# Gate weights loaded one step ahead of their product, into two buffers, over the scan's sixteen units

## The chip, the core and the metric

One core of a Trainium2 chip runs the whole layer. The engines are TensorE (PE in the profile; its weight loads are PEld), VectorE (DVE), ScalarE (ACT), GpSimd (POOL) and SyncE (SP), whose queue issues every DMA of this kernel. The metric is the device time of one execution in microseconds (us).

## What is computed

One layer of a hybrid backbone on 512 tokens of width 2048, with 256 context tokens, in float32. Cut to what matters here:

```
shift, scale, gate = split(silu(c) @ w_mod + b_mod, 3)
p = (rmsnorm(x, norm_g) * (1 + scale) + shift) @ w_in      # q, k, v, g, z, x|B|C, dt
y = bi_ssd(conv_silu(x|B|C), softplus(dt), ...)             # scan, both directions, 4 groups, 16 heads
a = windowed_gqa(rope(q), rope(k), v, context k and v, sink)
h = concat(rmsnorm(a * silu(g)), rmsnorm(y * silu(z)))
out = rmsnorm(x + gate * (h @ w_out), final_norm_g)
```

`gate` is a row of 2048 numbers, a product of one vector with a 2048 x 2048 part of `w_mod`. It is needed only in the output projection, at the end.

## The kernel before

Every product with weights runs on TensorE in three parts (hi x hi, lo x hi, hi x lo), so each weight block is split first: ScalarE rounds it to `wh` (L308), VectorE forms the rest `wl` (L310, counted under the helper's L55). Weights of the input projection come in units of 128 columns (`load_unit`, L298): two loads of 512 KB (`wr`, L303, two buffers), each split in two quarters (four buffers of `wh` and `wl`). Unit 0 is the last z block. Units 1 to 16 belong to the scan: for each of four groups two units of x, one of B, one of C (L598). Units 17 and 18 are the keys, then come queries and gates of the attention. x, B, k units multiply latent and context tokens (`pj` and `pjc` in the profile), C and q units the latent tokens alone.

After the four units of a group its scan follows (`ssd_group`, L474): the convolutions (L465 to L472), transposes, the chain of chunk states (`stc`, `stx`, L515 to L531), and for each of two head pairs the decays `df` (DMA broadcast L562, four buffers; ScalarE exp L563, L569, L573; VectorE L566, L575) and the output `yps` on TensorE (L586), which waits for them. While a scan runs, TensorE fills its time with the next group's first units, so much of them as its order allows.

The gate row is worked off in 64 steps among all this (`gate_step`, L274), one for each quarter of the units 2 to 17 (L311). A step loads 128 x 512 weights (`wg`, L289, 256 KB, **one** buffer) and adds their product with one column of silu(c) to an accumulator `ga` on VectorE (L290). The load is queued on SP behind the unit's own weight load (`issue_after`). Sixteen steps make one accumulator of 512 columns; after the sixteenth TensorE sums it over partitions (`gp`, L293), ScalarE copies the row (L294), SP stores it (L295), and POOL clears the one accumulator buffer for the next (L283).

A planner of the language fixes at build time the order of every engine's queue: each engine takes the earliest instruction of the program that is ready by the planner's own estimate of durations. `high_priority` puts weights (L301, by 200 instructions), convolutions (L461, 200) and the `df` loads (L561, 150) ahead. On the chip each queue then runs strictly in that order: an instruction that waits holds all behind it on its engine.

Of the kernel before, what the change touches and what calls it, by code (L numbers as in the profile page):

```python
# [6 lines left out]
F32 = mybir.dt.float32  # L7
# [5 lines left out]
PSUM = bass.MemoryType.PSUM  # L13

P = 128
D = 2048
KT = 16
# [6 lines left out]
GB = 1  # L24
# [11 lines left out]

# columns of the packed constants
C_ID, C_SEL, C_AP, C_AN, C_TRI, C_TRIT, C_MF, C_MB, C_END = 0, 128, 130, 258, 386, 514, 642, 770, 898
# columns of the packed small parameters
V_NG, V_BSH, V_BSC, V_CW, V_CB, V_DSK, V_AG, V_SG, V_DTB, V_ALOG, V_SINK, V_C, V_END = (  # L40
# [3 lines left out]
def emit(tc, xin, ctxT, wmod, wgate, bgate, wz, wvd, wu, wo, fng, vecs, cst, rope, out, dbg=None):  # L44
    nc = tc.nc
# [17 lines left out]
    with es:  # L63
# [7 lines left out]

# [1 line left out]
        c_sb = pc.tile([P, P + 2], F32, name="c_sb")  # L73
# [13 lines left out]

        # persistent activations: transposed normalised inputs in two exact parts
        cy = es.enter_context(tc.tile_pool(name="cy", bufs=1))
# [17 lines left out]
        def silu2(src, o, tmp):  # L107
            """o = 2 * src * sigmoid(src) = src * (1 + tanh(src / 2))"""
            nc.scalar.activation(tmp, src, AF.Tanh, scale=0.5)
            nc.vector.scalar_tensor_tensor(out=o, in0=tmp, scalar=1.0, in1=src, op0=ALU.add, op1=ALU.mult)  # L110

# [1 line left out]
        sus = ExitStack()  # L113
        su = sus.enter_context(tc.tile_pool(name="su", bufs=2, side="right", reuse_waits="tile"))

        def rms_rows(o, acc, n, tag):
            """1 / rms of every token, on all partitions, from the sums of squares per partition."""
            nt = n // P
            tot = bank(tag, f"rtot_{n}", shape=(P, nt))
            for t in range(nt):  # L120
                mm(tot[:, t:t + 1], acc[:, t * P:(t + 1) * P], ones[:, 0:1], True, True)
            rs = sp.tile([P, nt], F32, tag="rsc", name=f"rs_{n}")
            rstd_of(rs, tot, D)
            rps = bank(tag, f"rps_{n}", shape=(P, n))
            for t in range(nt):
                dg = sp.tile([P, P], F32, tag="dg", name=f"dg_{n}_{t}", bufs=4)
                nc.vector.tensor_scalar(out=dg, in0=ident, scalar1=rs[:, t:t + 1], scalar2=None, op0=ALU.mult)
                mm(rps[:, t * P:(t + 1) * P], ones, dg, True, True)
            nc.scalar.activation(o, rps, AF.Copy)

        def load_latent():
            """Latent tokens: transposed as they come, in column blocks; 1 / rms of every token on all partitions."""
            xtags = ["mm", "sa", "tp", "mm", "sa", "tp", "mm"]
# [3 lines left out]
            for q in range(4):  # L137
# [8 lines left out]
                for i in range(4):  # L146
                    k = 4 * q + i
# [28 lines left out]

        # silu of the two modulation vectors, zero-padded to one column group
        scp = su.tile([P, KT, 32], F32, tag="scp", name="scp", bufs=1)
# [87 lines left out]

# [1 line left out]
        dp = es.enter_context(tc.tile_pool(name="dp", bufs=1, space=bass.MemoryType.DRAM))  # L268
        grow = dp.tile([1, D], F32, name="grow")
        gsteps = iter(range(4 * KT))  # L270
        gacc = []
        geng = nc.vector

        def gate_step(ld):  # L274
            """One k block of 512 gate columns: products per partition, summed over partitions after the last."""
            i = next(gsteps, None)
            if i is None:
                return
            n, k = divmod(i, KT)
            if k == 0:  # L280
                ga = wp.tile([P, 512], F32, tag="ga", name=f"ga_{n}", bufs=1)
                gacc.append(ga)
                nc.gpsimd.memset(ga, 0.0)  # L283
                with tc.issue_after(ld.ins):
                    nc.sync.dma_start(ga[0:1, :], bgate[:, n * 512:(n + 1) * 512])
            ga = gacc[n]
            wg = wp.tile([P, 512], F32, tag="wg", name=f"wg_{n}_{k}", bufs=GB)
            with tc.issue_after(ld.ins):
                nc.sync.dma_start(wg, wgate[n, k])  # L289
            geng.scalar_tensor_tensor(out=ga, in0=wg, scalar=sc0[:, k:k + 1], in1=ga, op0=ALU.mult, op1=ALU.add)  # L290
            if k == KT - 1:
                gp = bank("tp", f"gp_{n}", shape=(1, 512))
                mm(gp, ones[:, 0:1], ga, True, True)  # L293
                nc.scalar.activation(ga[0:1, :], gp, AF.Copy)  # L294
                nc.sync.dma_start(grow[:, n * 512:(n + 1) * 512], ga[0:1, :])  # L295

# [1 line left out]
        def load_unit(u, ctxp=False):  # L298
            """Yields (k, hi, lo) weight blocks [128, 128] of unit u."""
            for hf in range(2):  # L300
                with tc.high_priority(HP_W):  # L301
                    wr = wp.tile([P, 8, P], F32, tag="wr", name=f"wr_{u}_{hf}", bufs=WR)
                    ld = nc.sync.dma_start(wr, wu[u, :, hf * 8:hf * 8 + 8, :])  # L303
                for qf in range(2):
                    with tc.high_priority(HP_W):
                        wh = wp.tile([P, 4, P], F32R, tag="wh", name=f"wh_{u}_{hf}_{qf}", bufs=4)
                        rr = wr[:, qf * 4:qf * 4 + 4, :]
                        nc.scalar.activation(wh, rr, AF.Copy)  # L308
                        wl = wp.tile([P, 4, P], F32R, tag="wl", name=f"wl_{u}_{hf}_{qf}", bufs=4)
                        tt(nc.vector, wl, rr, f32(wh), ALU.subtract)  # L310
                    if 2 <= u < 18:  # L311
                        gate_step(ld)
                    for i in range(4):
                        yield hf * 8 + qf * 4 + i, wh[:, i, :], wl[:, i, :]
# [14 lines left out]

# [1 line left out]
        def xtk(t, k):  # L331
# [61 lines left out]

# [1 line left out]
        sst = ExitStack()  # L395
# [6 lines left out]
        def w2(name, tag="w2", bufs=4, shape=(P, S)):  # L402
            return sd.tile(list(shape), F32, tag=tag, name=name, bufs=bufs)
# [5 lines left out]

        # dt: softplus(u) = max(u,0) + log1p(exp(-|u|)), log1p(e) = 2 atanh(e / (2 + e))  # L410
        fl = [P, 192]
# [47 lines left out]
        def conv_silu(pa, pb, ci, o):  # L459
            """Depthwise conv of width 3 and silu: pa [128, n] in PSUM -> o in SBUF."""  # L460
            with tc.high_priority(HP_CONV):  # L461
# [12 lines left out]
        def ssd_group(g, units):  # L474
# [65 lines left out]
            for pr in range(2):  # L540
                tix = 2 * g + pr
                # state term of both heads at once: exp(cs) scales it afterwards
                zs = []
# [9 lines left out]
                for hh in range(2):  # L553
# [3 lines left out]
                    for d in range(2):  # L557
                        # the row of running sums on all partitions; the differences take its place
                        df = w2(f"df_{r}_{d}", "df", DF)
# [20 lines left out]
                    dm.append(dx[0])  # L580
                # the two heads' products alternate between the two column halves of the array
                for c in range(NT):
# [12 lines left out]

        # units: (xs0 xs1 B C) x 4, k0 k1, q x 8, g x 8
        U0 = 8 - NZ
# [9 lines left out]

# [1 line left out]
        ast = ExitStack()  # L609
# [18 lines left out]

        # keys: scaled by 1/8 once (exact)
        kT = [a2(f"kT_{i}", "kT", 2, (P, S + CT)) for i in range(2)]  # L630
# [6 lines left out]

        # context activations are no longer needed: their room takes the SSD hi part and the attention output
        attT = [cy.tile([P, 2, S], F32, tag=f"cb{j}", name=f"at{j}") for j in range(4)]
        rsum = pc.tile([P, 2, NT], F32, name="rsum")  # L640

        def finish_half(src, hi_pair, goff, which, lo_tiles, pool, tag, bufs, apool, atag):
            """Sum of squares per token; norm gain; split in two parts."""
            acc = apool.tile([P, S], F32, tag=atag, name=f"hacc_{which}")
# [139 lines left out]

# [1 line left out]
        px_s.close()  # L786
# [12 lines left out]
        def add_x(n):  # L799
            """part = part * gate + x for 512 columns"""  # L800
            nn = slice(n * 512, (n + 1) * 512)
# [8 lines left out]
        for half in (1, 0):  # L810
# [6 lines left out]
            for n in range(4):  # L817
# [45 lines left out]
                for t in range(NT):  # L863
# [4 lines left out]
                    if last:  # L868
                        tmp = fp.tile([P, 512], F32, tag="xo", name=f"lt_{t}", bufs=4)
                        rt = rf[:, t:t + 1]  # L870
                        # the very last block in two column halves, so that only the second one's epilogue is left over
                        cut = [0, 512] if t < NT - 1 else [0, TC, 512]
# [137 lines left out]
```

## Time and profile before

| | us |
|---|---|
| median of 3 runs | 1056.75 |
| lowest, highest | 1056.4, 1060.85 |
| span of the profiled execution | 1054.8 |
| TensorE busy in that span | 1009.6 |
| VectorE busy | 722.0 |
| ScalarE busy | 494.6 |

The profiled execution's own time is its span, from its first to its last instruction; the median of the runs is 1.95 us above it, for what lies around the span. TensorE's busy time is modelled from its pipeline, so the idle time and the granted clock of a stretch say more than the share. In the rows below a bracket after a row of a timeline gives the engine's idle time before that row and what ended it.

### The profile page before, as it was taken

The page shows a single profiled execution, that of the slowest core. Times are in us where ns is not written, and L with a number is a line of the kernel's source. Part 1 is how long each engine was busy: PE and PEld are TensorE (multiplying, and loading weights), DVE is VectorE, ACT ScalarE, POOL GpSimd, SP SyncE. Part 2 cuts the span into 40 slices and gives each one's busy share as a digit, 9 for nine tenths or more (in the row PEclk, how much of TensorE's full clock was granted, in tenths as well). Part 3 has the DMA queues.
Part 4 walks back from the last instruction along what each step waited for, and adds up shares of the span by engine and source line. Part 5 has one row for each costly group of instructions (what it writes and reads, how often), then busy time and mean ns, then how long its engine had stood idle before and what let it go on. Part 6 is the DMA issues. An engine that isn't in the chain of part 4 may idle for free.

```text
span 1054.8 us, 15524 instructions
## 1 busy us (share of the span) xinstructions
PE 1009.6 (96%) x5682; PEld 818.7 (78%) x5682; DVE 722.0 (68%) x1474; ACT 494.6 (47%) x1064; POOL 173.5 (16%) x120
## 2 busy tenths in 40 slices
PE   5999999999999989989989999999999998999996
PEld 4677789788778868868868777777777777888885
DVE  4332378585875985885889888788798866333765
ACT  6222275263352453263345567666666655333333
POOL 1232200000210110110037100000000008744220
PEclk9999999999999999989999999999999999999998
DMA  9999963354244244444331211112111135442304
GB/s 333 385 347 348 343 212 95 110 165 147 70 120 145 92 149 125 112 120 139 120 107 56 84 61 42 59 40 80 41 40 61 61 99 221 151 167 91 100 33 160
DMA packets 50845, 143.25 MB, mean 136 GB/s; under 512 B 5544, under 2 KB 5928, under 8 KB 50512
## 3 DMA queue, kind: packets, MB, share of 16 engines
q1 hardware_dynamic: 50768, 142.25, 40.5%
q8 instruction: 45, 0.74, 0.3%
q14 instruction: 32, 0.26, 0.1%
HBM read 137.96 MB, written 4.27 MB: 135 GB/s over the span
## 4 chain that ended last, share of the span: by engine, by line
PE 61%; DVE 12%; DMA 5%; ACT 3%; issue 3%; POOL 1%; SPq 0%; ACTq 0%; DVEq 0%; POOLq 0%
PE pj L49 25%; PE o L49 14%; PE pjc L49 5%; PE pv L49 3%; PE ptp L756 3%; PE sl L49 3%; DMA wg<-in_wgate_dram 2%; PE vps L49 2%; DVE df L566 2%; DVE wl L55 2%; DMA df<-csd 2%; PE sc L49 2%; DVE ga L290 1%; DVE df L575 1%; PE stx L49 1%
## 5 line engine op out<-in xcount | busy, mean ns | idle before, releaser
L49 PE MATMUL pj<-xh,wh 128*128 128x512 f32 x560 | 225.5, 403 | 0.0
L49 PE MATMUL pj<-xl,wh 128*128 128x512 f32 x560 | 224.6, 401 | 0.0
L49 PE MATMUL pj<-xh,wl 128*128 128x512 f32 x560 | 224.0, 400 | 0.0
L308 ACT ACTIVATE wh<-wr 128x512 fp32r<-128x512 f32 x140 | 87.9, 630 | 137.5 <-PE pjc L49 66.2
L49 PEld LDWEIGHTS pj<-xh,wl 128*128 128x128 f32 x560 | 105.7, 189 | 21.3 <-issue 0.9
L55 DVE TENSOR_TENSOR wl<-wr,wh 128x512 fp32r<-128x512 f32 x140 | 103.5, 742 | 24.9 <-ACT wh L308 21.0
L49 PEld LDWEIGHTS pj<-xl,wh 128*128 128x128 f32 x560 | 106.4, 190 | 15.1 <-issue 1.9
L49 PEld LDWEIGHTS pj<-xh,wh 128*128 128x128 f32 x560 | 106.5, 190 | 13.9 <-issue 1.0
L55 DVE TENSOR_TENSOR wol<-wo,woh 128x512 fp32r<-128x512 f32 x56 | 53.3, 968 | 63.6 <-ACT woh L846 57.3
L290 DVE SCALAR_TENSOR_TENSOR ga<-wg,sc,ga 128x512 f32<-128x512 f32 x64 | 50.8, 794 | 49.2 <-DMA wg<-in_wgate_dram 48.1
L55 POOL TENSOR_TENSOR ec<-ec,ec 128x512 f32<-128x512 f32 x8 | 11.2, 1397 | 349.2 <-DVE ec L55 328.9
L846 ACT ACTIVATE woh<-wo 128x512 fp32r<-128x512 f32 x56 | 34.8, 630 | 70.8 <-PE o L49 62.3
L55 POOL TENSOR_TENSOR hacc<-hacc,hsq 128x512 f32<-128x512 f32 x14 | 20.4, 1454 | 288.7 <-ACT hsq L654 286.3
L49 PE MATMUL pjc<-chq,wh 128*128 128x256 f32 x224 | 65.2, 291 | 2.1 <-DVE xs L468 2.1
L49 PE MATMUL pjc<-clq,wh 128*128 128x256 f32 x224 | 64.4, 288 | 0.0
L49 PE MATMUL pjc<-chq,wl 128*128 128x256 f32 x224 | 63.7, 284 | 0.0
L760 ACT ACTIVATE ph<-ptp 128x512 fp32r<-128x512 f32 x72 | 41.1, 597 | 28.2 <-PE ptp L756 26.8
L49 PE MATMUL o<-woh,hsh 128*128 128x512 f32 x128 | 50.9, 397 | 3.1 <-ACT part L865 3.1
L55 DVE TENSOR_TENSOR pl<-ptp,ph 128x512 fp32r<-128x512 f32 x72 | 48.4, 683 | 7.8 <-ACT ph L760 7.4
L566 DVE SCALAR_TENSOR_TENSOR df<-df,cs,cs_sb 128x128 f32<-128x128 f32 x128 | 48.3, 433 | 4.6 <-ACT ec L563 4.5
L49 PEld LDWEIGHTS pjc<-chq,wh 128*128 128x128 f32 x224 | 42.2, 189 | 11.5 <-ACT ec L563 1.6
L55 POOL TENSOR_TENSOR wsl<-wsr,wsh 128x896 fp32r<-128x896 f32 x16 | 33.9, 2116 | 101.0 <-ACT wsh L231 95.7
(282 smaller groups left out, 2341.8 us busy)
## 6 DMA issues: line engine op xcount, KB each, us to landing
wr<-in_wu_dram SPq DMA_DIRECT2D x70, 512.0 KB, 3.9
wm<-in_wmod_dram SPq DMA_DIRECT2D x64, 512.0 KB, 7.5
wg<-in_wgate_dram SPq DMA_DIRECT2D x64, 256.0 KB, 2.6
wo<-in_wo_dram SPq DMA_DIRECT2D x32, 512.0 KB, 4.5
df<-csd SPq DMA_DIRECT2D x32, 256.0 KB, 4.1
wsr<-in_wz_dram SPq DMA_DIRECT2D x16, 448.0 KB, 6.6
wr_v<-in_wvd_dram SPq DMA_DIRECT2D x16, 288.0 KB, 2.9
xt<-in_xin_dram SPq DMA_DIRECT2D x8, 512.0 KB, 7.5
```

The lines of the kernel that those rows point to most:

```text
L49: return nc.tensor.matmul(o, l, r, start=start, stop=stop)
L55: eng.tensor_tensor(out=o, in0=a, in1=b, op=op)
L290: geng.scalar_tensor_tensor(out=ga, in0=wg, scalar=sc0[:, k:k + 1], in1=ga, op0=ALU.mult, op1=ALU.add)
L308: nc.scalar.activation(wh, rr, AF.Copy)
L566: nc.vector.scalar_tensor_tensor(out=df[:, cc], in0=bc[:, cc], scalar=cs[:, d, c, r:r + 1], in1=mF if d == 0 else mB, op0=ALU.subtract, op ...
L575: nc.vector.scalar_tensor_tensor(out=dx[0][:, cc], in0=df[:, cc], scalar=dtt[:, d, c, r:r + 1], in1=dx[0][:, cc], op0=ALU.mult, op1=ALU.add)
L756: nc.tensor.transpose(tp[:, i * P:(i + 1) * P], pt[i][:, n * P:(n + 1) * P], ident)
L760: nc.scalar.activation(ph, tp, AF.Copy)
L846: nc.scalar.activation(wh, wr[:, i, :], AF.Copy)
```

## The change

The steps start with unit 1 and end with unit 16, so that all 64 lie in the scan's units. A step no longer loads its own weights: the first step loads those of steps 0 and 1, and step i loads those of step i + 1, until all 64 are loaded. Even steps use the buffer that was there, odd ones a second buffer of the same size in the scan's own pool `sd`, which exists from the end of the start-up pools (L392) to the end of the last scan (L606). Products, sums and stores are the same. The remaining lines of the diff only drop comments.

```diff
-        gacc = []
+        gacc, gw = [], []
+
+        def gbuf(odd, name):
+            if odd:
+                return w2(name, "wg", 1)
+            return wp.tile([P, 512], F32, tag="wg", name=name, bufs=GB)
+
@@
             ga = gacc[n]
-            wg = wp.tile([P, 512], F32, tag="wg", name=f"wg_{n}_{k}", bufs=GB)
-            with tc.issue_after(ld.ins):
-                nc.sync.dma_start(wg, wgate[n, k])
+            for ii in range(len(gw), min(i + 2, 4 * KT)):
+                n_, k_ = divmod(ii, KT)
+                gw.append(gbuf(ii % 2, f"wg_{n_}_{k_}"))
+                with tc.issue_after(ld.ins):
+                    nc.sync.dma_start(gw[ii], wgate[n_, k_])
+            wg = gw[i]
             geng.scalar_tensor_tensor(out=ga, in0=wg, scalar=sc0[:, k:k + 1], in1=ga, op0=ALU.mult, op1=ALU.add)
@@
-                    if 2 <= u < 18:
+                    if 1 <= u < 17:
                         gate_step(ld)
```

## Rows read from the trace of the kernel before

**Rows 1.** The page's first part: busy us, share of the span, instructions of each engine.

```profile
PE 1009.6 (96%) x5682; PEld 818.7 (78%) x5682; DVE 722.0 (68%) x1474; ACT 494.6 (47%) x1064; POOL 173.5 (16%) x120
```

**Rows 2.** Busy time by stretch: length, PE, PEld, DVE, ACT, POOL, clock, DMA.

```profile
183.00:250.00 67.00, 64.63 (x355) 55.44 (x354) 41.47 (x94) 28.15 (x53) 0.00 (x0) 1.00 0.43 135
250.00:316.00 66.00, 61.82 (x353) 51.38 (x352) 52.56 (x113) 30.85 (x62) 8.46 (x7) 0.97 0.36 108
398.00:482.00 84.00, 79.45 (x450) 66.44 (x449) 63.78 (x130) 35.58 (x69) 8.58 (x7) 0.96 0.44 126
590.00:866.00 276.00, 275.19 (x1461) 216.48 (x1461) 227.29 (x549) 171.51 (x451) 0.00 (x0) 1.00 0.17 54
```

**Rows 3.** Waits of PE, 183 to 548 us: total us, times, longest.

```profile
PE yps L49 <- DVE df L55: 13.6, 4, 4.0
PE pjc L49 <- DVE xs L468: 2.1, 2, 1.2
PE gp L49 <- DVE ga L290: 1.9, 1, 1.9
PE csp L49 <- DVE da L432: 1.5, 1, 1.5
PE stc L49 <- ACT btok L504: 0.7, 1, 0.7
```

**Rows 4.** All waits, whole span; then tile wg: products (ns, first and last), landing.

```profile
DVE ga L290 <- DMA wg<-in_wgate_dram: 48.1, 29, 2.9
...
ACT ec L563 <- DMA df<-csd: 18.6, 10, 5.1
...
ACT wh L308 <- DMA wr<-in_wu_dram: 6.0, 4, 4.8
...
L290 DVE SCALAR_TENSOR_TENSOR ga<-wg,sc,ga x64: 737/750/1750, 195.8 to 544.1; 128x512 f32<-128x512 f32 x64
...
DMA to landing us min/median/max: 2.5/2.6/4.1
```

**Rows 5.** Timeline of DVE, end of group 2's projection, and one row of 202 us.

```profile
202.61 0.75 DVE L290 SCALAR_TENSOR_TENSOR ga<-wg,sc,ga 128x512 f32<-128x512 f32 x1 [1.33 <-DMA wg<-in_wgate_dram]
...
422.44 0.75 DVE L290 SCALAR_TENSOR_TENSOR ga<-wg,sc,ga 128x512 f32<-128x512 f32 x1 [1.23 <-DMA wg<-in_wgate_dram]
...
426.94 0.75 DVE L290 SCALAR_TENSOR_TENSOR ga<-wg,sc,ga 128x512 f32<-128x512 f32 x1 [2.92 <-DMA wg<-in_wgate_dram]
...
430.32 0.74 DVE L290 SCALAR_TENSOR_TENSOR ga<-wg,sc,ga 128x512 f32<-128x512 f32 x1
```

**Rows 6.** Busy time in the four scans, first conv of C to last yps.

```profile
262.00:291.50 29.50, 26.51 (x167) 21.67 (x166) 26.33 (x60) 11.52 (x24) 5.34 (x4) 1.00 0.23 73
345.40:374.40 29.00, 26.08 (x167) 22.11 (x167) 28.25 (x62) 10.91 (x22) 5.43 (x4) 1.00 0.32 101
428.20:460.00 31.80, 27.25 (x172) 23.20 (x171) 30.40 (x65) 11.48 (x23) 5.49 (x4) 0.98 0.39 108
511.60:543.50 31.90, 27.91 (x178) 23.73 (x178) 30.29 (x63) 10.14 (x21) 5.57 (x4) 1.00 0.32 98
```

**Rows 7.** The same stretches, L290 alone: length, DVE busy (products), clock, DMA.

```profile
262.00:291.50 29.50, 0.29 (x1) 1.00 0.23 73
345.40:374.40 29.00, 2.76 (x4) 1.00 0.32 101
428.20:460.00 31.80, 4.51 (x5) 0.98 0.39 108
511.60:543.50 31.90, 5.66 (x5) 1.00 0.32 98
```

**Rows 8.** Short stretches around the four waits of yps, columns as in rows 2.

```profile
291.40:294.90 3.50, 3.46 (x21) 2.96 (x22) 1.69 (x5) 1.21 (x3) 0.48 (x1) 0.51 0.36 93
374.00:377.40 3.40, 3.07 (x27) 2.67 (x28) 2.69 (x8) 0.80 (x2) 0.63 (x1) 1.00 0.70 193
458.70:465.50 6.80, 5.50 (x23) 3.20 (x24) 4.73 (x11) 1.66 (x3) 2.44 (x2) 0.50 0.54 138
544.00:547.40 3.40, 3.40 (x15) 1.28 (x11) 2.80 (x3) 0.63 (x1) 1.44 (x2) 0.50 0.00 0
```

**Rows 9.** Timelines of POOL and DVE in the last scan.

```profile
526.99 1.27 POOL L55 TENSOR_TENSOR ec<-ec,ec 128x512 f32<-128x512 f32 x1 [59.81 <-DVE ec L55]
...
527.14 1.66 DVE L290 SCALAR_TENSOR_TENSOR ga<-wg,sc,ga 128x512 f32<-128x512 f32 x1 [0.30 <-DMA wg<-in_wgate_dram]
```

**Rows 10.** SP's own waits, whole span: total us, times, longest.

```profile
SPq L289 <- DVE ga L290: 57.1, 51, 6.3
```

## The prediction

> **What bounds the kernel now.** I read the page's busy shares first: TensorE is busy 96% of the span, VectorE 68% [rows 1]. So the gate's products, which run on VectorE, are worth only what TensorE waits for. Next the stretches: the attention leaves TensorE under 1 us idle in 276, while the scan's part, 183 to 548 us, leaves 2.4 us idle in its first 67, 4.2 in the next 66, 4.6 in the 84 of group 2 [rows 2]. The list of TensorE's waits there sums to 13.6 + 2.1 + 1.9 + 1.5 + 0.7 = 19.8 us [rows 3]: that is all that this change can win directly, plus what the clock loses after such waits. Then the gate's own wait: VectorE sits 48.1 us before products whose weights haven't landed, 29 times, at most 2.9 us each; a load lands 2.6 us after its issue [rows 4]. The reader is to see that 48.1 is not the prize. Most of it lies where the row at 426.94 lies: in a projection, with TensorE supplied and VectorE waiting for nothing more urgent [rows 5]. TensorE is hungry elsewhere, at the end of each scan, where `yps` waits for VectorE's decays: four waits, 13.6 us [rows 3]. From the first convolution of C to that `yps` the four scans take 29.5, 29.0, 31.8 and 31.9 us, with VectorE busy 26.3, 28.3, 30.4 and 30.3 of it [rows 6], of which the gate's products are 0.29, 2.76, 4.51 and 5.66 [rows 7]. VectorE bounds these stretches, and the two with most products are the longest.
>
> **The change, part by part.** The profiled execution is 1054.8 us; the median of the runs is 1.95 above, and I add that back at the end.
>
> *Counts.* 64 loads of 256 KB and 64 products stay. Nothing is added to VectorE's work; a product beside nothing else costs 0.75 us [rows 5].
>
> *The load moves one step ahead.* Load i + 1 is issued in step i and must wait for product i - 1, the last reader of its buffer. Before, load i waited for the same product. So SP's wait for products (57.1 us in 51 waits [rows 10]) isn't removed, only used one step earlier. Behind it on SP stand the weight loads `wr` and the `df` broadcasts; those who wait for them lose 6.0 us (ScalarE's rounding) and 18.6 us (its exp) [rows 4], and I leave both as they are: bounds -2 to +2 us, a tenth of the 18.6, taken at zero since the same product releases SP. What changes is the rate: one step took load plus product plus issue, 426.94 - 422.44 = 4.5 us [rows 5], so four steps took 18 us, about as long as a unit, and the steps lagged behind their unit into the scan. With two buffers a product finds its weights landed, the 48.1 us of waits go, and the steps keep up with the weight loads.
>
> *The start.* At 202.61 a product held VectorE 1.33 us [rows 5] in the chain that makes the running sums, for which TensorE then waited 1.5 us [rows 3]. That goes: -1.3. Unit 1's four products now come here too; three of them in the chain would cost 3 x 0.75 = 2.25. Bounds -1.5 to +2.25; I take -1.3, because VectorE is idle 25 of 67 us here [rows 2].
>
> *The ends of the four accumulators* move from units 5, 9, 13, 17 to 4, 8, 12, 16, thus ahead of each scan. `gp` on TensorE costs what it did; its one wait for a product, 1.9 us [rows 3], lay in a scan and goes: -1.9 (bounds -1.9 to 0). ScalarE's copy, SP's store and POOL's clearing move along; POOL does nothing ahead of a scan (idle 59.8 us [rows 9]), so the clearing is covered. If that cover is gone, step 16 of each accumulator is late, and nobody waits for it but the next step.
>
> *The scans.* The last one has no unit left that brings products, so its 5.66 us [rows 7] should go nearly all: it can shrink from 31.9 to the 29.5 that the first takes almost without products, 2.4 us, at most to the wait itself, 4.0. In the third, two of the five products are late ones of unit 12 (counted through, the 41st to 44th of the 64; the 43rd starts at 430.32 [rows 5]); without them 1.5 us less (bounds 0 to 2.3, the first scan's length). In the first, products of unit 6 now come in, up to four; the second scan holds four products and is no longer than the first [rows 6, 7], since the first leaves VectorE 3.2 us idle, so I take 0 (bounds 0 to +2.4, the third's length). The second stays.
>
> *What is late next.* The length of a scan is not yet TensorE's wait. Its queue has `yps` where the planner thought the decays would be ready; if it reckons them earlier it puts `yps` earlier. I therefore count half of 2.4 + 1.5: -2.0 (bounds -6.3 to +2.4).
>
> *The clock.* Around the ends of the first, third and fourth wait of `yps` the granted clock was about 0.5, the lower level of 1.2 GHz, for 3.5, 6.8 and 3.4 us, in which TensorE was busy 3.5, 5.5 and 3.4; around the second's it stayed at 1.00, the level of 2.4 GHz [rows 8]. Half of that busy time is lost: 6.2 us in all. The waits that I expect to shrink carry 2.75 + 1.7 = 4.4; I take a quarter, -1.1 (bounds -6.2 to +1.7, one drop more, after the second scan).
>
> *One rule weighed.* A product beside POOL's addition took 1.66 us, against 0.75 alone [rows 9, 5]. The Trainium skill, SBUF — State Buffer, section "Who interferes with whom", says that a VectorE instruction with two SBUF inputs contends with a GpSimd instruction that reads SBUF, and that whoever issues first holds the shared ports for its whole instruction. The trace agrees with its 1.66 us. By that rule each product that enters a scan beside POOL costs 0.91 more than the plain price; with it, four products in the first scan would cost up to 3.6 us more than the sum has.
>
> *Sum.* -1.3 - 1.9 - 2.0 - 1.1 = -6.3: the span goes to 1048.5, the time to 1050.4. With the likely spread of the terms this case lies between 1046 and 1053.
>
> **The rivals.**
>
> *The waits were cover.* VectorE's 48.1 us are slack in the projections, the planner moves `yps` up as far as the decays come earlier, and only the wait of `gp` goes: -1.9, 1054.9. For it: no wait of TensorE for `wl`, the work that products hold up most, is in the list [rows 3]. Against it: the third and fourth scans are longer by what their products take [rows 6, 7].
>
> *It doesn't do what it says.* The load of step i + 1 stands on SP behind a wait for product i - 1, and behind `df` and `wr` loads that wait for VectorE. If the planner queues it just ahead of its product, VectorE waits as before: 1056.7. For it: SP already waits 57.1 us for products [rows 10]. Against: the even buffer no longer has to be read before the odd one is filled.
>
> *The products crowd the scans (slower).* With weights always landed, the planner can put products into each hole that it sees on VectorE in a scan: the eight of the next group's two x units, where now stand 1, 4, 5 and 5 [rows 7]. In the first three scans eight products of 0.75, two of them at 1.66, are 7.8 us [rows 5, 9], against 0.29, 2.76 and 4.51: +15.9. VectorE's idle time there takes 3.2 + 0.8 + 1.4 = 5.4 [rows 6], the last scan gives 2.4 and `gp` 1.9 back: +6.2. One clock drop more, +1.7: +7.9, 1064.7. For it: VectorE is the bound there. Against: a product is queued behind its unit's weight load, and only some of these loads are in by then. It decides from about six products in a scan.
>
> *All of TensorE's waits close.* If VectorE gets ahead everywhere, half of 19.8 + 6.2 goes: -13, 1043.8. Against: `yps` waited 3.0 us even in the first scan, with no product in it but the end of one [rows 7].
>
> **How the numbers follow.** Chances: forecast 0.50 (of it 0.35 beyond 0.5%), all waits close 0.10, waits were cover 0.18, doesn't do what it says 0.09, crowded scans 0.13. The measurement tells about 0.5% from no change, 5.3 us, thus below 1051.5 and above 1062.0. Faster 0.35 + 0.10 = 0.45; same 0.15 + 0.18 + 0.09 = 0.42; slower 0.13. The range 1043.5 to 1061.5 leaves out about half of the case at 1043.8 and most of the crowded one, under 0.2 in all. The predicted time is the forecast's, 1050.4.
>
> **What would show it.** In the profile after: VectorE's wait for `wg` near zero instead of 48.1 us; the first product some 10 us or more before 195.8, where it was [rows 4]; the last well before the last scan's `yps`, with at most one product in that scan; `gp` ahead of each scan and no wait of `gp` for a product; the four waits of `yps` below 13.6 us in all; fewer stretches at a granted clock of 0.5. I am wrong if the waits for `wg` go and TensorE's waits still sum to 19 us or more (then they were cover), if the first scans hold six or more products each (crowded), or if the time moves in a stretch after 548 us, where no product is left: that would be a new order of the queues, which no row here prices.

## The result

The changed kernel is **slower**: 1070.16 us (median of 4 runs, 1065.12 to 1072.57) against 1057.28 for the kernel before beside it, ratio 1.0113 [1.0093, 1.0134]. The forecast was 1050.4, its range ended at 1061.5, and slower had a chance of 0.13. The profiled execution after has a span of 1070.8 us, 16.0 more than before's 1054.8.

Did the change do what it says? It did. The rows that answer to [rows 1, 4], the page's first part, then waits and the tile `wg`:

```profile
PE 1018.5 (95%) x5682; PEld 826.5 (77%) x5682; DVE 719.1 (67%) x1474; ACT 493.9 (46%) x1064; POOL 175.6 (16%) x120
...
ACT ec L572 <- DMA df<-csd: 29.3, 15, 3.8
...
DVE ga L299 <- DMA wg<-in_wgate_dram: 19.9, 15, 3.1
...
L299 DVE SCALAR_TENSOR_TENSOR ga<-wg,sc,ga x64: 735/746/1854, 162.4 to 503.0; 128x512 f32<-128x512 f32 x64
...
DMA to landing us min/median/max: 2.5/3.9/6.2
```

VectorE's wait for gate weights fell from 48.1 to 19.9 us, although a load now lands 3.9 us after its issue instead of 2.6; the first product came 33 us earlier and the last 41 us earlier. VectorE does no more than before (719.1 us busy against 722.0), yet TensorE shows 8.9 us more busy time for the same 5682 instructions: it ran longer at the low clock. And ScalarE's wait for the rows of running sums (`df`) grew from 18.6 to 29.3.

TensorE's waits from 183 to 600 us, to be laid beside [rows 3], and the stretches of [rows 2]:

```profile
PE yps L49 <- DVE df L55: 14.0, 4, 3.6
PE pjc L49 <- DVE xs L477: 8.9, 4, 3.8
PE csp L49 <- DVE da L441: 2.2, 1, 2.2
```

```profile
183.00:250.00 67.00, 60.81 (x322) 52.20 (x321) 42.44 (x100) 26.67 (x50) 0.00 (x0) 0.95 0.45 135
250.00:316.00 66.00, 62.49 (x359) 52.13 (x358) 49.54 (x94) 23.92 (x44) 9.37 (x7) 0.97 0.38 116
398.00:482.00 84.00, 79.81 (x456) 66.90 (x455) 62.80 (x131) 35.27 (x68) 9.44 (x7) 0.98 0.41 126
590.00:866.00 276.00, 274.71 (x1459) 216.33 (x1458) 233.68 (x555) 171.08 (x450) 8.44 (x6) 1.00 0.17 56
```

The wait of `gp` is gone, the four waits of `yps` didn't shrink (13.6 to 14.0), and a wait that was small before grew fourfold: the context half of a projection (`pjc`) waits for VectorE to finish the convolution of `xs`, which holds the PSUM bank (the buffer for TensorE's results) that it needs: 2.1 to 8.9 us. The first stretch shows most: TensorE idle 6.2 us instead of 2.4, at a mean clock of 0.95 instead of 1.00.

Where the time is lost, by the start of the same work in both traces (after minus before): first product of unit 0 +2.0, sums of the decays' inputs (`csp`) +4.5, second x convolution of group 0 +7.2, its C convolution +9.6, the C convolution of group 1 +10.5, of group 2 +12.3, of group 3 +16.3, first scores of the attention +14.3, last ones +14.5, last product of all +16.0. So most of the loss is in the scan's part, the larger share of it in group 0. But 2.0 us are there as it begins, 1.5 of them in two waits of the v product ahead of it (`vps`) that the trace before doesn't have, and 1.5 more come in the output projection.

**The bookkeeping.** I added up, from 100 to 1040 us, TensorE's waits (over 0.1 us each) and the time at which the trace has the clock at 0.5 of full speed, the level of 1.2 GHz. Before: 24.3 us of waits, 13.7 us at half clock. After: 31.2 and 34.1. If half of the time at half clock is lost, that makes 6.9 + 10.2 = 17.1 us, where the spans differ by 16.0. In each of the kernels below whose profile can be used, the same sum gives the span's difference from before within 2 us; it is the yardstick of this document. Waits and clock are those of one profiled execution each, the ratios those of all runs:

| kernel | time ratio [interval] | waits | of it `pjc` | of it `yps` | at half clock |
|---|---|---|---|---|---|
| before | 1 | 24.3 | 2.1 | 13.6 | 13.7 |
| after | 1.0113 [1.0093, 1.0134] | 31.2 | 8.9 | 14.0 | 34.1 |
| shift_alone | 1.0079 [1.0053, 1.0106] | 29.2 | 8.0 | 8.8 | 23.9 |
| ahead_alone | 1.0014 [1.0000, 1.0028] | 22.5 | 3.3 | 12.1 | 17.1 |
| pad_alone | 0.9996 [0.9982, 1.0010] | 24.1 | 3.2 | 13.7 | 10.2 |
| own_step_two_buffers | 1.0108 [1.0077, 1.0139] | 29.1 | 8.5 | 13.6 | 30.7 |
| ahead_from_unit_2 | 1.0109 [1.0081, 1.0137] | 29.9 | 9.1 | 13.7 | 27.3 |
| one_buffer_from_unit_2 | 1.0088 [1.0067, 1.0109] | 31.7 | 12.8 | 6.1 | 10.2 |
| four_more_at_start | 0.9996 [0.9980, 1.0012] | 20.5 | 0.2 | 13.6 | 13.7 |
| no_gate | 0.9958 [0.9942, 0.9974] | | | | |
| after_held | 1.0116 [1.0093, 1.0140] | 31.0 | 10.0 | 13.7 | 20.5 |
| held_from_unit_2 | 1.0110 [1.0091, 1.0129] | 30.0 | 9.4 | 13.6 | 27.3 |
| b_and_c_units | 1.0071 [1.0049, 1.0092] | 26.9 | 8.2 | 13.8 | 27.3 |
| second_accumulator | 0.9989 [0.9976, 1.0002] | 23.2 | 5.5 | 11.0 | 17.1 |
| x1_four_more | 1.0068 [1.0043, 1.0094] | 25.1 | 4.2 | 12.0 | 30.7 |
| b_four_more | 1.0065 [1.0041, 1.0089] | 25.1 | 4.8 | 12.1 | 23.9 |
| x1_products_short | 1.0099 [1.0083, 1.0114] | 27.7 | 6.9 | 13.7 | 27.3 |
| ends_in_unit_17 | 1.0108 [1.0090, 1.0126] | 29.7 | 8.9 | 13.3 | 30.7 |
| no_weight_loads | 1.0010 [0.9993, 1.0026] | 22.5 | 2.1 | 13.3 | 17.1 |
| sums_on_pool_queue | 1.0282 [1.0252, 1.0312] | 40.6 | 13.5 | 18.7 | 47.8 |

The profiled execution of no_gate was a disturbed one, so only its time is used.

**One such wait, read through four queues.** Group 0 of the kernel after, around the 3.8 us. TensorE ends the second x unit at 234.3; its next `pjc` starts at 241.16. Timelines of SP, VectorE, ScalarE and TensorE (start, length, engine, line, instruction; in brackets idle before it, and what ended it):

```profile
228.44 0.33 SPq L297 DMA_DIRECT2D wg<-in_wgate_dram  x1
229.31 0.33 SPq L312 DMA_DIRECT2D wr<-in_wu_dram  x1
230.42 2.49 SPq L297 DMA_DIRECT2D wg<-in_wgate_dram  x2
232.96 0.42 SPq L571 DMA_DIRECT2D df<-csd  x1
```

```profile
227.66 0.75 DVE L299 SCALAR_TENSOR_TENSOR ga<-wg,sc,ga 128x512 f32<-128x512 f32 x1 [1.30 <-DMA wg<-in_wgate_dram]
...
235.14 0.75 DVE L299 SCALAR_TENSOR_TENSOR ga<-wg,sc,ga 128x512 f32<-128x512 f32 x1 [1.12 <-DMA wg<-in_wgate_dram]
...
237.24 1.44 DVE L575 SCALAR_TENSOR_TENSOR df<-df,cs,cs_sb 128x128 f32<-128x128 f32 x5
238.60 0.61 DVE L584 SCALAR_TENSOR_TENSOR df<-df,dtt,df 128x128 f32<-128x128 f32 x2
239.21 0.75 DVE L475 SCALAR_TENSOR_TENSOR xs<-pj,v_sb,xs 128x511 f32<-128x511 f32 x1
```

```profile
237.14 0.63 ACT L572 ACTIVATE ec<-df 64x512 f32<-64x512 f32 x1 [1.94 <-DMA df<-csd]
...
238.42 0.76 ACT L474 ACTIVATE xs<-pj,v_sb 128x512 f32<-128x512 f32 x1
```

```profile
241.16 0.55 PE L49 MATMUL pjc<-chq,wh 128*128 128x256 f32 x1 [3.83 <-DVE xs L477]
```

Two weight loads hold SP from 230.42 to 232.91; from 228 to 233.2 it waits at such loads 1.6 us for products on VectorE, whose buffers they need, and, by the trace, 1.1 us for a decay there. The `df` load stands behind them. So ScalarE gets that row at 237.14, and the convolution of `xs`, whose input was ready at 234.3, starts only at 238.42, since it is queued behind. VectorE meanwhile stands in its own queue for gate weights, 1.30 and 1.12 us, with decays and its part of the convolution behind. TensorE then waits 3.83 us and loses the clock:

```profile
239.50:246.90 7.40, 5.74 (x22) 5.29 (x23) 4.92 (x11) 3.46 (x8) 0.00 (x0) 0.54 0.47 155
```

In the other three groups the way is another. There ScalarE's last wait before that convolution (1.14, 1.01 and 1.62 us) ends not with a row but with a decay on VectorE, queued behind a product that had waited 0.68, 0.55 and 1.17 us for its weights. Group 3, VectorE, then ScalarE:

```profile
491.72 0.75 DVE L299 SCALAR_TENSOR_TENSOR ga<-wg,sc,ga 128x512 f32<-128x512 f32 x1 [1.17 <-DMA wg<-in_wgate_dram]
492.39 0.34 DVE L575 SCALAR_TENSOR_TENSOR df<-df,cs,cs_sb 128x128 f32<-128x128 f32 x1
```

```profile
492.77 0.63 ACT L578 ACTIVATE df<-df 128x512 f32<-128x512 f32 x1 [1.62 <-DVE df L575]
```

The `pjc` waits of these groups are 1.64, 0.52 and 2.90 us, so VectorE's waits for weights are at most 2.4 of their 5.1.

These readings are chains of rows. Whether they are the cause is what the experiments are for. The theories they set apart, as they arose: the **start** (unit 1's products in the chain of the running sums), the **crowded scans**, the **layout** of the added buffer, the **end of the gate** with unit 16, a **crowded x1 stretch** (VectorE between the convolutions of a group's two x units, with the next scan's decays in it), and the **loads** in the queues.

### The profile page after: what moved, and what is told of

It reads as the page before. It is cut to its first block, busy times and chain, and to the rows that moved or that the text cites. A ratio compares the mean times of both kernels' runs of the same rounds, so it can differ in the third digit from the quotient of the medians.

```text
span 1070.8 us, 15500 instructions
## 1 busy us (share of the span) xinstructions
PE 1018.5 (95%) x5682; PEld 826.5 (77%) x5682; DVE 719.1 (67%) x1474; ACT 493.9 (46%) x1064; POOL 175.6 (16%) x120
## 4 chain that ended last, share of the span: by engine, by line
PE 74%; DVE 9%; DMA 8%; ACT 4%; issue 3%; POOL 1%; SPq 0%; ACTq 0%; DVEq 0%; POOLq 0%
PE pj L49 27%; PE o L49 14%; PE zps L49 7%; PE pjc L49 4%; DMA wg<-in_wgate_dram 3%; PE md L49 3%; PE pv L49 3%; PE ptp L765 3%; PE vps L49 3%; PE sl L49 3%; DMA df<-csd 3%; DVE df L575 2%; PE sc L49 2%; DVE ga L299 1%; DVE df L584 1%
## 5 line engine op out<-in xcount | busy, mean ns | idle before, releaser
L49 PE MATMUL pjc<-chq,wh 128*128 128x256 f32 x224 | 68.1, 304 | 8.9 <-DVE xs L477 8.9
L49 PE MATMUL pjc<-clq,wh 128*128 128x256 f32 x224 | 67.0, 299 | 0.0
L299 DVE SCALAR_TENSOR_TENSOR ga<-wg,sc,ga 128x512 f32<-128x512 f32 x64 | 51.1, 798 | 20.2 <-DMA wg<-in_wgate_dram 19.9
L49 PEld LDWEIGHTS pjc<-chq,wh 128*128 128x128 f32 x224 | 44.5, 198 | 19.2 <-issue 6.3
L49 PE MATMUL o<-woh,hsl 128*128 128x512 f32 x128 | 51.3, 401 | 0.0
L49 PEld LDWEIGHTS pjc<-clq,wh 128*128 128x128 f32 x224 | 44.5, 199 | 8.7
L49 PE MATMUL o<-wol,hsh 128*128 128x512 f32 x128 | 50.7, 396 | 0.0
```

Source lines behind the costliest of these rows:

```text
L49: return nc.tensor.matmul(o, l, r, start=start, stop=stop)
```

## The experiments

### The two halves of the change, and the room

shift_alone is the kernel before with one line changed:

```diff
-                    if 2 <= u < 18:
+                    if 1 <= u < 17:
```

ahead_alone is the kernel after on units 2 to 17, the last four steps with one buffer. pad_alone is the kernel before with 2 KB more in the pool `sd`. own_step_two_buffers is the kernel after, each step loading its own weights:

```diff
-            for ii in range(len(gw), min(i + 2, 4 * KT)):
+            for ii in range(i, i + 1):
```

> The kernel before with its steps in units 1 to 16, still one buffer and each load in its own step. The changed kernel lost 1.1% (1057.3 to 1070.2 us). If the shift makes the loss (products and loads now stand in the first 30 us of the scan's part, where the running sums and the first decays are made), this takes 1065 to 1072 us, with the first conv of unit 2 some 5 us or more later than before. If the second buffer and the earlier load make it, this takes 1054 to 1060 us.

> Two buffers and the load one step ahead, but steps in units 2 to 17 as before; the last four steps, of unit 17, use the old buffer and load in their own step, since the second buffer's pool ends with unit 16. If loading ahead makes the loss, 1065 to 1072 us, with TensorE's waits for the convolutions' PSUM banks near the 8.9 us of the changed kernel (2.1 before). If the shift makes it, 1050 to 1059 us: the waits for weights go and the scans keep their order.

> The kernel before with an unused 2 KB per partition in the scan's pool, cleared once on GpSimd, so that all tiles of the pool lie where they lie in the changed kernel; every other engine's queue is in the order of before. If where the tiles lie, or the room taken from the pool before, costs time, 1062 us or more. If not, 1055 to 1059 us.

> The changed kernel (units 1 to 16, two buffers), but each step loads its own weights. If the loss comes from loading one step ahead as such, 1056 to 1061 us. If it comes from the second buffer (products can follow each other closely) or from the shift, 1065 to 1072 us as in the changed kernel.

Measured 1.0079, 1.0014, 0.9996 and 1.0108. The layout is out. Loading ahead isn't the loss: on units 2 to 17 it costs 0.14%, at most 0.28%, and without it two buffers on units 1 to 16 lose as much as the whole change. It is the shift by one unit that loses, with either number of buffers. ahead_alone also settles what a scan without products is worth, products (L299) in its four scans, then TensorE's waits:

```profile
263.30:293.90 30.60, 0.00 (x0) 1.00 0.20 66
345.40:375.90 30.50, 0.00 (x0) 1.00 0.21 62
427.80:458.30 30.50, 0.00 (x0) 1.00 0.20 65
511.00:541.10 30.10, 0.23 (x1) 1.00 0.18 58
```

```profile
PE yps L49 <- DVE df L55: 12.1, 4, 3.0
PE pjc L49 <- DVE xs L477: 3.3, 4, 1.8
```

No product in them, and `yps` still waits 3.0 us each time: of the 13.6 us in [rows 3] only 1.5 went with the products.

### The start

ahead_from_unit_2 is the kernel after without unit 1, unit 3 with two steps per quarter. one_buffer_from_unit_2 is the same on the kernel before (units 2 to 16). four_more_at_start is the kernel before with four loads and products of weight zero added in unit 1. no_gate is the kernel before without the 64 steps.

```diff
-                    if 1 <= u < 17:
+                    if 2 <= u < 17:
+                        gate_step(ld)
+                    if u == 3:
                         gate_step(ld)
```

> The changed kernel (two buffers, one step ahead, no step in unit 17), but without steps in unit 1: unit 3 takes two in each quarter instead. Theory start (the four steps of unit 1 push back the running sums, the first decays and the first convolutions): 1055 to 1061 us, with the running sums within 2.5 us of where loading ahead in units 2 to 17 had them, 211.4. Theory phase (all later products standing one unit earlier against the scans makes most of the loss): 1064 to 1071 us.

> The kernel before with no steps in unit 17; unit 3 takes two in each quarter instead; one buffer, each load in its own step. Theory start: 1054 to 1059 us, as before. Theory phase, or that the end at unit 16 costs: near the 1064.6 us of the shift alone, 1061 us or more.

> The kernel before with four more loads and four more products of weight zero, in unit 1; the 64 steps stay in units 2 to 17. Theory start: the running sums come some 4 us later, 1059 to 1065 us. Theory phase: the four cost what the cover allows, 1056 to 1058 us.

> All 64 steps left out; the gate is the bias row alone, so this leaves out the product of silu(c) with its weights. It says what the steps cost in all. If the waits of the outputs for decays come from the products, they fall well below 13.6 us in the four scans and the time below 1045 us. If the planner places the outputs as early as it thinks the decays ready, whatever else VectorE does, these waits stay near 3 us each and the time falls by 10 us at most.

Measured 1.0109, 1.0088, 0.9996 and 0.9958. The start theory falls twice: without unit 1 the loss stays, and four steps more in unit 1 cost nothing. no_gate bounds the whole matter: all 64 loads and products together cost the kernel before 0.42%, 4.4 us, so 13 us can hardly be the price of the work; what is left is the order in which it stands. one_buffer_from_unit_2 loses in another place, the last scans (37 to 44 us long, with VectorE idle 6 to 14 us of each), where single-buffered products wait for weights ahead of the decays.

### The scans

after_held makes POOL's clearing of each accumulator wait, in the planned order, for the last addition of the scan before, so no product can enter a scan. held_from_unit_2 is the same without unit 1. b_and_c_units is the kernel after with two steps per quarter in the B and C units and none in the x units. second_accumulator is the kernel before with a second buffer for the second accumulator.

```diff
-                nc.gpsimd.memset(ga, 0.0)
+                if scans:
+                    with tc.issue_after(scans[-1].ins):
+                        nc.gpsimd.memset(ga, 0.0)
+                else:
+                    nc.gpsimd.memset(ga, 0.0)
```

> The changed kernel with one edge of order more: the clearing of each accumulator but the first is queued on GpSimd behind the last operation of the scan before it, so the eight products of the next two units can't come into that scan. Theory crowded scans (eight products in each of three scans): three scans go from 32.3 to 30 us and less TensorE time waits for convolutions; 1056 to 1062 us. If what costs is the start (unit 1) or anything else of the shift, 1065 to 1071 us as in the changed kernel.

> The same edge of order in the variant without steps in unit 1 (unit 3 takes two in each quarter), 1067.6 us without the edge. Theory crowded scans: 1055 to 1060 us, as loading ahead in units 2 to 17 (1057.8), which has no product in a scan. Difference to the held changed kernel: what the four steps of unit 1 cost at the start, 0 to 4 us.

> The changed kernel with two steps in each quarter of the B and C units and none in the x units. In the planner's order each of the first three scans then holds 2 products instead of 8, and none stands in the first 30 us. Theory crowded scans: 1055 to 1061 us. If the shift costs by something else, 1064 us or more.

> The kernel before, units 2 to 17, one weight buffer, with a second accumulator buffer for the second set of 16 steps, which takes the wait for the first accumulator away. In the planner's order the first scan then holds 4 products instead of none, the third none instead of 6. Theory crowded scans: no more products in scans than before, and about the same time, 1054 to 1060 us; the first scan becomes longer by some 2 us, the third shorter.

Measured 1.0116, 1.0110, 1.0071 and 0.9989. In the kernel after the first three scans hold eight products each:

```profile
270.40:303.60 33.20, 5.47 (x8) 1.00 0.36 105
354.30:387.50 33.20, 5.47 (x8) 0.99 0.35 105
438.40:471.70 33.30, 5.49 (x8) 1.00 0.35 105
526.30:557.00 30.70, 0.00 (x0) 1.00 0.19 56
```

in after_held they hold none, and are 2.7 us shorter (first of the four); the waits, though, only change place:

```profile
269.20:299.70 30.50, 0.00 (x0) 1.00 0.20 62
```

```profile
PE yps L49 <- DVE df L55: 13.7, 4, 3.5
PE pjc L49 <- DVE xs L481: 10.0, 6, 3.2
```

So crowded scans are real and are not the loss. second_accumulator is the nearest to a gain among the kernels that compute everything, and can't be told from the kernel before.

### Is it one stretch, or the end?

By now every losing kernel had more `pjc` waits. In those with two buffers the stretch ahead of them holds 6 to 8 products beside 20 to 27 decay operations; in ahead_alone, which doesn't lose, it is 7 beside 17 in groups 1 to 3. (The two losing kernels with one buffer hold 3 or 4 products there.) Two more things were still possible: that stretch's load on VectorE, and that the gate now ends with unit 16. x1_four_more and b_four_more add 16 products without loads to ahead_alone, in that stretch or (with units 5, 8, 12 and 16) in the next:

```diff
+        def dummy():
+            ga = gacc[-1]
+            geng.scalar_tensor_tensor(out=ga, in0=ga, scalar=0.0, in1=ga, op0=ALU.mult, op1=ALU.add)
...
                         gate_step(ld)
+                    if u in (4, 6, 10, 14):
+                        dummy()
```

x1_products_short narrows the products of that stretch in the kernel after; ends_in_unit_17 gives the kernel after four more steps of scalar zero in unit 17, with the last `gp` behind them:

```diff
-            geng.scalar_tensor_tensor(out=ga, in0=wg, scalar=sc0[:, k:k + 1], in1=ga, op0=ALU.mult, op1=ALU.add)
+            w = 32 if k in range(8, 15) else 512
+            geng.scalar_tensor_tensor(out=ga[:, 0:w], in0=wg[:, 0:w], scalar=sc0[:, k:k + 1], in1=ga[:, 0:w], op0=ALU.mult, op1=ALU.add)
```

> The kernel ahead_alone (two buffers, loaded ahead, units 2 to 17; 1057.8 us) with 16 more products of scalar zero on the accumulator itself, without a load, four in each stretch of VectorE's queue between the convolution of a group's first x unit and that of its second (the x1 stretch; 4 more than before in each, so 7 in group 0 and 11 or 12 in the others, beside 17 to 26 decay operations). Theory 'crowded x1 stretch': the stretch goes from 16.7 to 19 or 20 us, TensorE waits 2 to 4 us more per group for the convolution (pjc), mostly with a stretch at half clock behind it: 1065 to 1075. Theory 'it is the loads' (SyncE's queue, in which the rows of running sums stand behind the weights): no new load, so 1057 to 1060. Theory 'the gate ends too early' (with unit 16): it still ends in unit 17 here, 1057 to 1060.

> The same 16 products of scalar zero on ahead_alone, but queued between the second x unit's convolution and that of the B unit, where VectorE idled 6.4 to 8.5 us of 17: the control. 'Crowded x1 stretch': within 2 us of ahead_alone, 1056 to 1060, the x1 stretches stay at 16.7 to 19 us. If VectorE's time counts wherever it lies: as x1_four_more.

> The kernel after, with the products of the weight blocks 8 to 14 of each accumulator (those that stand in the x1 stretch) on 32 instead of 512 columns; so 480 columns of these seven blocks are left out of the gate. Loads, buffers and units 1 to 16 stay. 'Crowded x1 stretch': the waits for the second x unit's convolution (8.9 us) fall to about 2 and the clock drops behind them go, 12 to 15 us of the 13 lost come back: 1055 to 1060. 'It is the loads' and 'the gate ends too early': stays at 1066 to 1070.

> The kernel after with four more loads and products of scalar zero in unit 17, into the last accumulator, whose sum over partitions waits for them: the gate ends where it did before, and nothing else of it is moved. 'The gate ends too early': back to 1056 to 1059. 'Crowded x1 stretch' and 'it is the loads': 1068 to 1071.

Measured 1.0068, 1.0065, 1.0099 and 1.0108. The end of the gate is out. So is the crowded stretch: the same extra work costs as much one stretch later, and with the seven products of each x1 stretch taking 1.7 to 3.9 us instead of 5.2 to 6.3, and VectorE idle 4.3 to 5.1 us of it, the kernel after keeps most of its loss. What the narrow products left is shown by ScalarE in group 3 of x1_products_short:

```profile
487.58 0.62 ACT L318 ACTIVATE wh<-wr 128x512 fp32r<-128x512 f32 x1
490.52 0.63 ACT L573 ACTIVATE ec<-df 64x512 f32<-64x512 f32 x1 [2.32 <-DMA df<-csd]
491.06 0.76 ACT L475 ACTIVATE xs<-pj,v_sb 128x512 f32<-128x512 f32 x1
```

The convolution is late all the same, now behind a row of sums. The two additions also cost more, some 0.5% beside ahead_alone, than their 12 us of VectorE time should at the rate of no_gate (64 steps, 4.4 us): in both the waits grew by 2.6 us (25.1 against 22.5), and the clock took 6.8 and 3.4 us (30.7 and 23.9 us at half level against 17.1).

### The loads

no_weight_loads is the kernel after with no gate weights loaded, each product reading the accumulator in their place. sums_on_pool_queue is the kernel after with the `df` loads issued from POOL's queue:

```diff
-            for ii in range(len(gw), min(i + 2, 4 * KT)):
-                n_, k_ = divmod(ii, KT)
-                gw.append(gbuf(ii % 2, f"wg_{n_}_{k_}"))
-                with tc.issue_after(ld.ins):
-                    nc.sync.dma_start(gw[ii], wgate[n_, k_])
-            wg = gw[i]
-            geng.scalar_tensor_tensor(out=ga, in0=wg, scalar=sc0[:, k:k + 1], in1=ga, op0=ALU.mult, op1=ALU.add)
+            geng.scalar_tensor_tensor(out=ga, in0=ga, scalar=sc0[:, k:k + 1], in1=ga, op0=ALU.mult, op1=ALU.add)
```

```diff
-                            nc.sync.dma_start(df, csd[d * 16 + r].partition_broadcast(P))
+                            nc.gpsimd.dma_start(df, csd[d * 16 + r].partition_broadcast(P))
```

> The kernel after without the 64 weight loads: each product reads the accumulator in place of the weights (so the gate is left out; the 64 products, the clears, the sums over partitions and the stores stay, in units 1 to 16, with 8 products in each of the first three scans). Theory 'in-order queues around the loads' (VectorE stands in its queue for weights, SyncE for buffers, and the rows of running sums, ScalarE's work on them and the second x unit's convolution stand behind both): TensorE's waits for that convolution fall from 8.9 to 3 us or less, and most of the stretches at half clock behind them go: 1054 to 1059. Theory 'VectorE's time wherever it lies' (x1_four_more, b_four_more): 1064 to 1070.

> The kernel after, with one change: the 32 loads of the rows of running sums (df) are issued from POOL's queue instead of SyncE's, so none of them stands behind a weight load. VectorE's order keeps 97 lines of 1340 different, all in the order of decays and products. If it is SyncE's queue that makes the rows late: ScalarE's waits for them fall from 29.3 to under 8 us, the waits for the second x unit's convolution from 8.9 to 3 to 5: 1056 to 1062. If it is VectorE's own waits for weights, or its time: 1065 to 1071, with the waits for the rows gone and the convolution still late. A price of its own is possible, where a load on POOL stands behind POOL's additions of the scan.

Measured 1.0010 [0.9993, 1.0026] and 1.0282. Without the loads the loss is gone, with all 64 products, the shift, the clears and the sums in place, and with **more** products in the first three scans than the kernel after has (products alone, then TensorE's and one of ScalarE's waits):

```profile
263.50:297.40 33.90, 7.70 (x9) 1.00 0.20 57
345.70:379.50 33.80, 7.61 (x9) 1.00 0.18 57
427.50:461.40 33.90, 7.58 (x9) 1.00 0.19 57
```

```profile
PE yps L49 <- DVE df L55: 13.3, 4, 3.5
PE pjc L49 <- DVE xs L471: 2.1, 3, 1.5
...
ACT ec L566 <- DMA df<-csd: 28.1, 15, 3.7
```

The waits of `pjc` are back at the 2.1 us of [rows 3]. ScalarE still waits 28.1 us for rows of sums, as after (29.3), so those waits alone don't make the loss. Two reservations: with the loads gone the planner's order moved too (the first sixteen products all run ahead of group 0's x1 stretch; groups 1 to 3 kept seven there, beside 23 decay operations instead of 26), and the kernel has no traffic for gate weights, 16 MB less. Neither was taken away by itself, so that the queues and not one of these make the loss is argued and not shown.

sums_on_pool_queue was to part the two queues and didn't, because it brought a price of its own. Waits of ScalarE and POOL:

```profile
POOL df L571 <- DVE xs L475: 82.2, 1, 82.2
...
POOL df L571 <- ACT wh L317: 42.7, 9, 10.3
ACT ec L572 <- DMA df<-csd: 40.8, 20, 4.3
```

POOL now stands in its queue before loads that aren't free to go, with its additions behind them, and the rows come later than in the kernel after (40.8 against 29.3). The direction fits, rows later by 11.5 us and `pjc` from 8.9 to 13.5, but it separates nothing.

## Why the prediction was wrong

**The step that failed** is the one on the loads: "The load moves one step ahead", where it says of those behind SP's waits "I leave both as they are: bounds -2 to +2 us ... taken at zero since the same product releases SP". Of the two waits meant there, ScalarE's for `wr` stayed (6.0 and 5.6 us), but its wait for `df` grew by 10.7 us, from 18.6 to 29.3. The reason given for the zero is about the step ahead, and that step cost next to nothing (ahead_alone, 1.0014). The shift of 64 loads and products by one unit, which the same diff makes, has no term among the loads, and alone it loses 0.79% (shift_alone). A loss of 0.7% or more is in every kernel of the table that loads and has its 64 steps done by unit 16, and absent in the one that doesn't load, with the reservations made there.

The term counted the loads at issue, from SP's side, and took their places among the `df` loads, the decays and the convolutions as fixed. As the timelines above read, three in-order queues (SP, VectorE, ScalarE) carry a delay from one to the next: in group 0 by a row late on SP, in the others by decays behind a product that waits for weights. These waits were to go; 19.9 of the 48.1 us remain. What was late next was not `yps`, at which the text looked, but the convolution that frees a PSUM bank for the next projection, at 2.1 us the second row of [rows 3], to which the sum gave no term: 8.9 us. In all the sum had -5.2 us for TensorE's waits and -1.1 for the clock; the profile has +6.9 and +10.2.

**The start** (-1.3, bounds -1.5 to +2.25): `csp` waits 2.2 instead of 1.5, within the bounds, on their bad side. But unit 1's products aren't why: they cost nothing in four_more_at_start, and the wait is 2.4 without them in ahead_alone and in ahead_from_unit_2.

**The wait of `gp`** (-1.9) went, as said.

**The scans** (-2.0): the last scan is 30.7 us long and without a product; the others grew to 33.2 with eight. These rows begin 0.8 us earlier than those of [rows 6], with ScalarE's part of the convolution; counted alike they are 29.9 us, nearly the 29.5 foreseen, and 32.3 to 32.5. Both hardly mattered, since `yps` waits 3.0 to 3.6 us at the end of a scan with none, with eight and with nine. The planner places `yps` where it expects the decays, which the text named as the doubt and still counted half for.

**The clock** (-1.1, at most +1.7): sized by drops behind `yps`. It came to (34.1 - 13.7) / 2 = +10.2 us, the larger half of the loss: the new `pjc` waits brought drops of their own (6.8 us each, at 240.1 and 496.1), all four `yps` waits were followed by one instead of three (17.1 us together, 13.7 before), and one of 3.4 us came at 905.7. This last one is luck: it follows a wait of 3.1 us in the output projection that the kernel before has too, without a drop.

**The rule weighed**, in timelines of VectorE and POOL of the kernel after:

```profile
307.35 0.74 DVE L299 SCALAR_TENSOR_TENSOR ga<-wg,sc,ga 128x512 f32<-128x512 f32 x1
...
309.30 1.85 DVE L299 SCALAR_TENSOR_TENSOR ga<-wg,sc,ga 128x512 f32<-128x512 f32 x1
```

```profile
307.57 1.66 POOL L55 TENSOR_TENSOR yt<-yt,ec 128x512 f32<-128x512 f32 x1 [7.03 <-DVE yt L600]
309.31 1.30 POOL L55 TENSOR_TENSOR y<-y,yt 128x512 f32<-128x512 f32 x1
```

The product that began ahead of POOL's addition took 0.74 us and the addition 1.66; the one that began with the next addition took 1.85 and that addition 1.30. The first pair agrees with the Trainium skill's rule (SBUF — State Buffer, "Who interferes with whom") that the one issued first goes through and the other is held up. The second shows a product held up, but its two starts are 0.01 us apart, too close to tell who came first. What this costs no run prices alone; no_weight_loads has such products too (1.85 us at 303.12) and loses nothing.

**The rivals.** *The waits were cover* was right on its mechanism: the wait for weights fell by 28 us and TensorE's waits still sum to 25.1, above the 19 that the text set as its mark. It had no place for a loss. *The products crowd the scans* was the only slower one, at 1064.7, and its mark, six products a scan, was passed; its time is the nearest. It was still the wrong reason, and the near time is luck: without products in the scans the ratio is 1.0116 (after_held), with nine and no loads there is no loss. *It doesn't do what it says* and *all waits close* are refuted by the waits for `wg` and for `yps`.

**What stays open.** Why the loads do no harm on units 2 to 17 and do on 1 to 16, in both cases with two buffers; how much goes through VectorE's waits for weights and how much through rows late behind SP; and whether the traffic of the weights or the planner's new order has a share of its own. In group 0 the `pjc` wait goes with VectorE's wait for weights in the x1 stretch in four kernels (0.8 us of it in ahead_alone, 1.5 in ahead_from_unit_2, 2.7 in after_held, 2.8 in after, with 1.8, 2.7, 3.2 and 3.8 of `pjc`), but not in own_step_two_buffers (2.1 with 1.8). Taking away these waits alone, with more buffers, was not tried.

## What to carry to other kernels

A wait that costs nothing where it stands (48 us here) is no measure of what moving it is worth; and a moved load takes its place ahead of other loads and work in queues that run in order, so list for each queue what ends up behind it, down to the instruction that frees a buffer for the busiest engine. Give every small wait of that engine a term of its own, not only the longest, because the second row may be the one that grows. To find out whether loads or arithmetic cost, take the loads away and leave the arithmetic: that one kernel told more here than all variations of the schedule, though the planner's order moved with it.

## What the hardware showed

TensorE's waits cost more than their length, and not in proportion. A wait of 2.2 us for `csp` left the clock at 1.00 in the kernel after, and the same wait of 2.2 us in own_step_two_buffers was followed by 3.4 us at 0.50, the lower of the two levels. The stretches of both, after's first:

```profile
211.00:217.50 6.50, 4.14 (x27) 3.60 (x27) 5.35 (x16) 1.41 (x4) 0.00 (x0) 1.00 0.59 186
```

```profile
213.80:217.20 3.40, 3.40 (x13) 2.78 (x12) 2.38 (x7) 1.17 (x3) 0.00 (x0) 0.50 0.52 154
```

Over these kernels the time at half level goes from 10.2 to 47.8 us, in pieces of 3.4 and 6.8. I had not expected that a kernel could lose more by the clock than by the waits (10.2 and 6.9 us here), nor that 16 products without a load, in stretches where VectorE had idled 5.9 us or more, cost some 0.5% (b_four_more, 1.0065, beside ahead_alone, 1.0014), more than half of it in this way.
